# Moving two output projections into their attentions' buffers, new buffers at the end of the latent stage, and a later transpose of the softmax maxima, in a two-layer diffusion backbone on one Trainium2 core

## The chip, the cores and the metric

The kernel runs on one core of a Trainium2 chip. A core has a matrix engine (TensorE, PE in the profile, with its weight loads shown apart as PEld), a vector engine (DVE), an activation engine (ACT), a general engine (POOL), and a queue engine (SP) that here issues transfers only. ACT and POOL issue some transfers too. Operands lie in an on-chip memory (SBUF), the matrix engine writes into accumulator banks (PSUM), and everything larger lives in device memory. The metric is the device time of one execution in microseconds (us), as the median of several runs. Three runs of the kernel before took 3708.83, 3715.74 and 3721.25 us, so its median is 3715.74 us.

## What is computed

The reference is a network of two layers over 2048 latent tokens on a grid 64 wide, with 256 context tokens ahead of them; a token has 1024 channels. Both layers normalize and modulate, project, mix, gate, project again and add to the stream:

```python
for i in range(DEPTH):                     # 2 layers
    h  = rms_norm(x,  norm_g[i]) * (1 + scale)   + shift
    hc = rms_norm(cx, norm_g[i]) * (1 + c_scale) + c_shift
    y, yc = even_mixer(...) if i % 2 == 0 else odd_mixer(...)
    x = x + gate * y
    if i < DEPTH - 1:                      # the context is updated by layer 0 only
        cx = cx + c_gate * yc
```

Layer 0 (even) has two heads' groups side by side: latent attention (8 heads, queries and keys of 96 elements made from low-rank latents, softmax over all 2304 tokens for latent queries and over the 256 context tokens for context queries) and a gated linear attention (4 heads, run in both directions). Layer 1 (odd) is a neighbourhood attention (16 heads, a window of 8 rows by 16 columns plus all context tokens). Both end with a product by a 1024 x 1024 matrix: `readout(...)` in layer 0 for 18 tiles of 128 tokens (2 of context, 16 latent), and `jnp.dot(o * silu(z), w_out)` in layer 1 for the 16 latent tiles.

## The kernel before, in words

All is in float32. A product is made of three matmuls on operands split into a high and a low part: high by high, high by low, low by high. Lines 120 to 122 and 129 to 131 issue them. The split of an operand is one copy on ACT (the high part) and one subtraction on DVE (the low part); `project_split` (line 1059) does it for a projection. Tokens come in 18 tiles of 128, of which tiles 0 and 1 are context.

The stages, with their times in the profiled execution:

- `even_latent`, to about 549 us. For each tile it makes the latents (`gemm`), then queries, keys and values from them (`up`: transposes at line 495 into the tag "tp", splits into `lth` and `ltl`, products into `qn`, `kn` and `vn`, and a chain of squares, sums and powers on ACT, DVE and POOL that normalizes `qn` and `kn`), and one step later transposes queries and keys (`fin`, line 549), splits them into `qkhl` (two buffers) at lines 106 and 553, and stores them to the device tensors `QT` and `KT`. At its end `first` computes four column blocks of the next stage's products, evicts each into the one buffer `vn` and stores it to `Un`.
- `even_rest`, to about 1099 us. The rest of layer 0's input products run as the main generator of `weave`, in steps of three matmuls; beside them the side generator `maxes` computes, head by head, all scores of the attention once (line 651) and reduces them to row maxima (line 652). After a head, its maxima are reduced to `mc` (line 655), transposed on PE (line 657), negated into `mr` and stored by POOL as one more row of `QT`, so that the attention can subtract them inside its product. `weave` starts the side after `head` main steps (20) and then issues 1.06 side steps for each main step.
- `even_mix`, to about 1981 us: both attentions of layer 0, in pools `atS` (SBUF) and `atP` (PSUM). `finish` (line 833) ends a block of 512 queries: a product that sums the softmax denominators (`den`, line 838), a logarithm and an exponential on ACT, three DVE operations, one on POOL, and a store to `RT`.
- The output projection of layer 0, to about 2197 us, by `project` (line 1080) in new pools `woS` and `woP`: `project_load` reads a tile of `RT` and of the stream, `project_split` splits it into `prh` and `prl`, `project_steps` issues 48 matmuls of 512 columns, multiplies by the gate on DVE (line 1072), adds on POOL (line 1073), and stores.
- `odd_qk` and `odd_vz`, to about 3110 us: the input products of layer 1. In `odd_vz` again a side generator `maxes` computes score maxima (line 1280, reductions at 1275 and 1286), with a transpose of `mc` at line 1293 and four stores by POOL for each head.
- `odd_attention`, to about 3498 us. The projections of its first two output tiles are issued inside its pools, to about 3527 us.
- The other 14 tiles by `project` in new pools `wpA`, `wpS` and `wpP`, to the end. Here `project_load` also reads the gate path `z` and POOL multiplies it in (line 1056).

The order of the work on an engine is the order in which the program issues it, except where a block asks for another place with `issue_after`, and the planner of the framework places instructions of a generator by priority. Buffers of a tag are reused in turn; whoever writes one next waits for its last reader. New pools that take the memory of earlier ones wait for those in the same way.

Of the kernel before, what the change touches and what calls it, by code (L numbers as in the profile page):

```python
# [10 lines left out]
F32 = mybir.dt.float32  # L11
# [77 lines left out]
class Kern:  # L89
# [303 lines left out]
    def even_latent(self, ws, wrest, kept):  # L393
# [5 lines left out]
        with ExitStack() as es:  # L399
# [87 lines left out]
            def up(t):  # L487
# [3 lines left out]
                for g in range(2):  # L491
                    ps = self.tl(pp, [P, 4, P], "tp")
# [49 lines left out]
            def fin(t):  # L542
                qn, kn = nat.pop(t)
                for z, (src, dst) in enumerate(((qn, self.QT), (kn, self.KT))):
                    col = 2 * z + (0 if t < NCT else 1)
                    for h2 in range(2):
                        ps = self.tl(pp, [P, 4, P], "tp")
                        for j in range(4):
                            nc.tensor.transpose(ps[:A_QK, j, :], src[:, h2 * 4 + j, :], self.ident[:])
                        hl = self.tl(sp, [P, 4, 2, P], "qkhl", F32R, bufs=2)  # L550
# [9 lines left out]

            def first(t, j):
                (hi, lo), (wh, wl) = kept[t], wrest[j]
                ps = self.tl(pp, [P, LAT_CHUNK], "gm", bufs=2)
                self.mm3(ps[:], (lambda k: hi[:, k, :], lambda k: lo[:, k, :]),
                         (lambda k: wh[:, k, :], lambda k: wl[:, k, :]), range(KD))
                u = self.tl(sp, [P, LAT_CHUNK], "vn", bufs=1)
                self.act(u[:], ps[:])
                nc.scalar.dma_start(self.Un[t, :, (j - 2) * LAT_CHUNK : (j - 1) * LAT_CHUNK], u[:])
# [31 lines left out]
    def even_rest(self, ws, win, hT):  # L600
        nc = self.nc
        self.zaT = self.scr("zaT", (4, P, T), F32)
        with ExitStack() as es:
# [33 lines left out]
            def maxes():  # L637
                for h in range(A_HEADS):
# [4 lines left out]
                    for t in range(NT):  # L643
# [4 lines left out]
                        for n, k0 in enumerate(range(0, lim, 512)):  # L648
# [4 lines left out]
                            yield mm  # L653
                    mc = self.tl(sp, [P, NT], "mc", bufs=1)
                    nc.vector.tensor_reduce(out=mc[:], in_=m[:], axis=AX.X, op=ALU.max)
                    ps = self.tl(pp, [P, 512], "mx", bufs=5)
                    mm = nc.tensor.transpose(ps[:NT, :P], mc[:], self.ident[:])
                    r = self.tl(sp, [P, P], "mr", F32R, bufs=1)
                    self.act(r[:NT], ps[:NT, :P], AF.Copy, scale=-1.0)
                    nc.gpsimd.dma_start(self.QT[h, 0, A_QK].rearrange("(t p) -> t p", p=P), r[:NT].bitcast(F32))  # L660
                    yield mm

            self.weave(gemms, maxes(), 1.06, 30, 20)
# [169 lines left out]
    def finish(self, av, dacc, zt, dst, w, ap, pp, tag, lnp=None, bufs=(1, 2), out=None):  # L833
# [3 lines left out]
        for h in range(2):  # L837
            nc.tensor.matmul(den[h * 64 : h * 64 + 64, :w], self.mtwos[:], dacc[h], start=True, stop=True)
# [12 lines left out]
    def even_attention(self, ap, pp):  # L851
# [4 lines left out]
        ring = [self.tl(ap, [P, 2, W], f"akh{n}", F32R, bufs=1) for n in range(4)]  # L856
        for kh in ring:
            nc.gpsimd.memset(kh[A_QK : A_QK + 1].bitcast(F32), 1.0)
# [65 lines left out]
        for j in range(4):  # L924
# [12 lines left out]
            for nb, (q0, w, kts) in enumerate(blocks):  # L937
# [18 lines left out]
                for n, kt in enumerate(kts):  # L956
# [21 lines left out]
                    if nb == 4 and j < 3 and n % TT == TT - 1 and n < NT - 1:  # L978
                        load(keys(j + 1, n // TT + 1), low(j + 1, n // TT))
        while pend:  # L980
# [10 lines left out]
    def even_mix(self, e1, win, hT):  # L991
# [3 lines left out]
        with ExitStack() as es:  # L995
            with ExitStack() as esa:
# [26 lines left out]
                for n, _ in enumerate(att):  # L1023
                    if n == 18:
                        pre = {t: self.project_load(self.RT, t, t, self.i["xin"], ld) for t in range(2)}
# [13 lines left out]
            gate = [self.gate_load(0, c, self.tl(sp, [P, D], f"gate{c}", bufs=1)[:]) for c in range(2)]  # L1039
            self.project(0, self.RT, [(t, t) for t in range(NT)], self.i["xin"], self.x1, w, sp, pp, ld, pre, gate, ahead=ahead())  # L1040
# [39 lines left out]
    def project(self, l, RT, tiles, xsrc, dst, w, sp, pp, ld, pre, gate, z=None, ahead=iter(())):  # L1080

        for t, o in tiles:
# [3 lines left out]
            for _ in self.project_steps(hi, lo, x, gate[1 if t < NCT else 0], w, lambda: self.tl(pp, [P, 512], "pj", bufs=4),  # L1086
# [127 lines left out]
    def odd_vz(self, ws, win, hT):  # L1214
# [3 lines left out]
        with ExitStack() as es:  # L1218
# [31 lines left out]
            def maxes():  # L1250
                for h in range(16):
# [11 lines left out]
                    for R in range(16):  # L1263
# [19 lines left out]
                        for ro, ri, rn in pieces("q", 0, g, r0, nr):  # L1283
                            for co, ci, cn in pieces("q", 1, c, c0, w):
# [3 lines left out]
                                n += 1  # L1288
                        yield mm
                    mc = self.tl(mp, [P, 16], "mc", bufs=1)  # L1290
                    nc.vector.tensor_reduce(out=mc[:], in_=m[:], axis=AX.X, op=ALU.max)
                    pt = self.tl(pp, [P, 512], "mx", bufs=5)
                    nc.tensor.transpose(pt[:16, :P], mc[:], self.ident[:])
                    r = self.tl(mp, [P, P], "mr", F32R, bufs=1)
                    self.act(r[:16], pt[:16, :P], AF.Copy, scale=-1.0)
                    for g in range(4):
# [402 lines left out]
```

## Time and profile before

| what | value |
|---|---|
| median of three runs | 3715.74 us |
| the profiled execution | 3709.59 us |
| its span on the core | 3707.8 us |
| PE busy | 3566.3 us (96%) |
| DVE busy | 2374.2 us (64%) |
| ACT busy | 1438.5 us (39%) |
| POOL busy | 1209.2 us (33%) |
| mean granted PE clock | 0.982 |

The span is the time from the first to the last instruction; the execution lasts 1.8 us longer. A view by windows gives each engine's busy time in a stretch; the timeline lists instructions with start and duration, and in square brackets the idle time of the engine ahead of one and what released it; the list of waits sums these by pair. Matmuls overlap, so the step from one start to the next, and not the duration shown, is what one costs.

### The profile page before, as it was taken

Reading aid. Unit: us, or ns where it says so; the run is one execution under the profiler, and the core shown is the slowest. Engines: PE = TensorE matmul, PEld = TensorE weight load, DVE = VectorE, ACT = ScalarE, POOL = GpSimd, SP = SyncE. Lnnn points to the kernel's source line nnn. Section 1 sums busy time; section 2 is a strip of 40 time slices with the busy share of each in tenths; the row PEclk is TensorE's granted clock in tenths of the full one; section 3 lists DMA queues with packets and bytes.
Section 4 is the critical chain, followed back from the end, with each engine's and each line's share of the span. In section 5 each row is a group of like instructions: output and inputs, shape, how many; then the busy total and the mean of one; then the engine's idle time right before and its main releaser. Section 6 shows DMA issues by size and latency. Waiting matters only on the chain.

```text
span 3707.8 us, 51752 instructions
## 1 busy us (share of the span) xinstructions
PE 3566.3 (96%) x18404; PEld 2754.6 (74%) x18404; DVE 2374.2 (64%) x4860; ACT 1438.5 (39%) x2741; POOL 1209.2 (33%) x1336
## 2 busy tenths in 40 slices
PE   7999989999999999999999999999899999999889
PEld 6988988888886666655656878888688887555567
DVE  4677656888876666697665344545478773666722
ACT  5545541111115555555553124444322223555400
POOL 1433420111111212122201233333344443777743
PEclk9999999999999999999999999999999999999999
DMA  7455453222242232334514543445744437887564
GB/s 257 138 164 160 129 170 98 87 75 85 75 127 63 82 97 79 91 105 121 163 55 151 165 149 117 150 142 175 215 143 123 136 117 200 216 215 205 162 195 130
DMA packets 364372, 512.18 MB, mean 138 GB/s; under 512 B 25826, under 2 KB 243890, under 8 KB 358211
## 3 DMA queue, kind: packets, MB, share of 16 engines
q1 hardware_dynamic: 322642, 425.49, 39.0%
q0 software_dynamic: 19872, 55.92, 5.1%
q10 hardware_dynamic: 21600, 27.46, 2.1%
q8 instruction: 146, 2.39, 0.3%
q14 instruction: 112, 0.91, 0.1%
HBM read 329.38 MB, written 179.37 MB: 137 GB/s over the span
## 4 chain that ended last, share of the span: by engine, by line
PE 79%; DVE 7%; DMA 6%; POOL 3%; ACT 3%; issue 2%; SPq 0%; POOLq 0%; ACTq 0%; DVEq 0%
PE gm L129 9%; PE gm L130 9%; PE gm L131 9%; PE av L905 7%; PE st L963 4%; PE mx L651 4%; PE st L964 3%; PE st L965 3%; PE pj L129 3%; PE pj L130 3%; PE pj L131 3%; PE o L1406 2%; PE st L1373 1%; DMA wraw<-w_od 1%; PE mx L1280 1%
## 5 line engine op out<-in xcount | busy, mean ns | idle before, releaser
L954 DVE TENSOR_TENSOR acc<-acc,apt 128x512 f32<-128x512 f32 x512 | 364.6, 737 | 158.3 <-ACT apt L106 155.4
L106 ACT ACTIVATE apt<-st 128x512 f32<-128x512 f32 (+1 forms) x592 | 344.4, 594 | 284.3 <-PE st L965 247.2
L652 DVE TENSOR_REDUCE mm<-mx 128x1 f32<-128x512 f32 (+1 forms) x656 | 389.3, 629 | 81.3 <-PE mx L651 74.4
L905 PE MATMUL av<-apt,av 128*64 128x512 f32 (+1 forms) x1184 | 288.0, 600 | 0.0
L963 PE MATMUL st<-aq,akh 97*128 97x512 f32 (+1 forms) x592 | 254.0, 429 | 5.1 <-ACT apt L106 2.8
L651 PE MATMUL mx<-mk,mq 96*128 96x512 f32 (+1 forms) x656 | 236.8, 373 | 6.1 <-DMA mq<-QT 4.6
L964 PE MATMUL st<-aq,akh 96*128 96x512 f32 (+1 forms) x592 | 235.2, 397 | 0.0
L965 PE MATMUL st<-aq,akl 96*128 96x512 f32 (+1 forms) x592 | 234.0, 396 | 0.0
L1286 DVE CUSTOM_DVE_ANT_1 mx<-mx,mtab 128x225 f32<-128x225 f32 (+12 forms) x576 | 183.7, 339 | 58.1 <-PE mx L1280 42.7
L106 ACT ACTIVATE u<-gm 128x352 f32<-128x352 f32 (+1 forms) x140 | 68.6, 497 | 369.4 <-PE gm L131 208.0
L905 PEld LDWEIGHTS av<-apt,av 128*64 128x64 f32 x1184 | 82.1, 138 | 157.1 <-issue 155.8
L1537 DVE TENSOR_TENSOR opt<-st,tab 128x64 f32<-128x64 f32 (+10 forms) x576 | 142.7, 316 | 86.6 <-PE st L1374 58.3
L963 PEld LDWEIGHTS st<-aq,akh 97*128 97x128 f32 x592 | 112.3, 190 | 98.4 <-issue 43.7
L1412 POOL TENSOR_TENSOR oacc<-oacc,opt 128x682 f32<-128x682 f32 (+9 forms) x144 | 169.6, 1206 | 23.2 <-ACT opt L106 21.9
L1073 POOL TENSOR_TENSOR px<-py,px 128x512 f32<-128x512 f32 x64 | 86.4, 1350 | 232.8 <-DVE py L1072 232.8
L106 ACT ACTIVATE opt<-opt 128x930 f32<-128x930 f32 (+8 forms) x130 | 104.4, 805 | 106.2 <-DVE opt L1537 102.3
L106 ACT ACTIVATE prh<-pr 128x1024 fp32r<-128x1024 f32 x32 | 33.9, 1058 | 263.1 <-PE pj L130 235.6
L651 PEld LDWEIGHTS mx<-mk,mq 96*128 96x128 f32 x656 | 121.7, 189 | 17.6 <-issue 5.0
L965 PEld LDWEIGHTS st<-aq,akl 96*128 96x128 f32 x592 | 113.6, 192 | 25.5
L964 PEld LDWEIGHTS st<-aq,akh 96*128 96x128 f32 x592 | 113.9, 192 | 18.0
L1373 PE MATMUL st<-q,kt 128*128 128x480 f32 (+5 forms) x256 | 99.0, 389 | 25.8 <-DVE opt L1537 20.9
L106 ACT ACTIVATE x<-px,modB,modA 128x128 f32<-128x128 f32 x272 | 99.3, 469 | 57.2 <-PE px L331 50.9
(517 smaller groups left out, 10069.0 us busy)
## 6 DMA issues: line engine op xcount, KB each, us to landing
q<-Q SPq DMA_DIRECT2D x48, 512.0 KB
H<-x ACTq DMA_DIRECT2D x36, 512.0 KB
adaw<-ada_w SPq DMA_DIRECT2D x64, 256.0 KB
x<-H SPq DMA_DIRECT2D x32, 512.0 KB
pr<-RT SPq DMA_DIRECT2D x32, 512.0 KB
wraw<-w_od SPq DMA_DIRECT2D x64, 256.0 KB
K1t<-okt POOLq DMA_DIRECT2D x32, 512.0 KB, 7.6
kt<-K1t SPq DMA_DIRECT2D x32, 512.0 KB
```

The costliest lines, as they stand in the source:

```text
L106: return self.nc.scalar.activation(out, in_, func, **kw)
L129: self.nc.tensor.matmul(out, lh(k), rh(k), start=j == 0, stop=False)
L130: self.nc.tensor.matmul(out, lh(k), rl(k), start=False, stop=False)
L131: yield self.nc.tensor.matmul(out, ll(k), rh(k), start=False, stop=j == n - 1)
L651: mm = nc.tensor.matmul(ps[:, :w], q[:A_QK, (t % 6) * P : (t % 6) * P + P], k[:A_QK, k0 : k0 + w], start=True, stop=True)
L652: nc.vector.tensor_reduce(out=m[:, t, n : n + 1], in_=ps[:, :w], axis=AX.X, op=ALU.max)
L905: nc.tensor.matmul(O[j, nb][i * 64 : i * 64 + 64, :w], V[j, kt // TT][:, kt % TT, i * 64 : i * 64 + 64], pts[i][:, :w], start=n == 0, stop ...
L954: nc.vector.tensor_tensor(out=acc[i][:, :w], in0=a[:, :w], in1=pts[i][:, :w], op=ALU.add)
L963: nc.tensor.matmul(ps[:, :w], kh[: A_QK + 1, i, kq], qh[: A_QK + 1, :w], start=True, stop=False)
L964: nc.tensor.matmul(ps[:, :w], kh[:A_QK, i, kq], ql[:A_QK, :w], start=False, stop=False)
L965: mm = nc.tensor.matmul(ps[:, :w], kl[:A_QK, i, kq], qh[:A_QK, :w], start=False, stop=True)
L1286: nc.vector.tensor_tensor_reduce(out=s, in0=s, in1=tb[:, ri : ri + rn, ci : ci + cn], scale=1.0, scalar=-3e38, op0=ALU.add, op1=ALU.max, a ...
```

## The change

It has four parts.

1. *End of the latent stage.* For the last tile, `up` transposes into the bank tag "px" and not "tp". `fin` of the last tile takes the keys first and puts their halves into `lth` and `ltl`, with transposes in "px"; the queries follow in "tp" and `qkhl`. `first` evicts into slices of a tile of the tag "u", three to a tile, and not into the one buffer `vn`.
2. *Maxima.* In both `maxes` the transpose of a head's maxima, its negation and its stores are put into a function `post`, called inside the next head (after its tile 3 in layer 0, at row block 4 in layer 1), and after the loop for the last head. In `even_rest` the side generator starts after 32 main steps, not 20.
3. *Layer 0's output projection.* Tiles 0 and 1, the context, are computed with the attention's buffers: the gate in `ring[0]`, the halves in the tag "aq", the banks "gl" and "st", the result in "rc". Nine of their matmuls stand ahead of the attention's last value products, the others behind the last `den`. Tile 2's loads are issued ahead of the new pools; `project` does tiles 2 to 17.
4. *Layer 1's output projection.* All tiles are computed inside the attention's pools. Operands of a tile come from the ring of the tag that `exps` takes, fetched two tiles ahead (`fetch`), multiplied and split one tile ahead (`ready`). The pools `wpA`, `wpS` and `wpP` are gone.

The diff, cut:

```diff
@@ even_latent: up, fin, first
-                    ps = self.tl(pp, [P, 4, P], "tp")
+                    ps = self.tl(pp, [P, 4, P], "px" if t == NT - 1 else "tp")
...
-                for z, (src, dst) in enumerate(((qn, self.QT), (kn, self.KT))):
+                both = [(0, qn, self.QT), (1, kn, self.KT)]
+                for z, src, dst in both[::-1] if t == NT - 1 else both:
...
-                        ps = self.tl(pp, [P, 4, P], "tp")
+                        ps = self.tl(pp, [P, 4, P], "px" if z and t == NT - 1 else "tp")
...
-                        hl = self.tl(sp, [P, 4, 2, P], "qkhl", F32R, bufs=2)
+                        if z and t == NT - 1:
+                            hl = self.tl(sp, [P, 8, P], ("lth", "ltl")[h2], F32R, bufs=1)[:].rearrange("p (j s) t -> p j s t", s=2)
+                        else:
+                            hl = self.tl(sp, [P, 4, 2, P], "qkhl", F32R, bufs=2)
...
+            spare = []
             def first(t, j):
+                if not spare:
+                    x = self.tl(sp, [P, LAT_COLS], "u", bufs=2)
+                    spare.extend(x[:, n * LAT_CHUNK : (n + 1) * LAT_CHUNK] for n in range(3))
...
-                u = self.tl(sp, [P, LAT_CHUNK], "vn", bufs=1)
-                self.act(u[:], ps[:])
+                u = spare.pop(0)
+                self.act(u, ps[:])
@@ even_rest: maxes (odd_vz alike, with "if R == 4 and post: post()")
+                        if t == 3 and post:
+                            yield post()
                     mc = self.tl(sp, [P, NT], "mc", bufs=1)
                     nc.vector.tensor_reduce(out=mc[:], in_=m[:], axis=AX.X, op=ALU.max)
+                    def post(h=h, mc=mc):
...
+                        return mm
+                yield post()
-            self.weave(gemms, maxes(), 1.06, 30, 20)
+            self.weave(gemms, maxes(), 1.06, 30, 32)
@@ even_mix
+                early = []
+                for n, last in enumerate(att):
                     if n == 18:
-                        pre = {t: self.project_load(self.RT, t, t, self.i["xin"], ld) for t in range(2)}
+                        gate = self.gate_load(0, 1, self.att_free[:].rearrange("p i w -> p (i w)")[:, :D].bitcast(F32))
+                        for t, tag in zip(range(NCT), (("gl", 2), ("st", 3))):
+                            r, x = self.project_load(self.RT, t, t, self.i["xin"], ld)
+                            hl = self.tl(ap, [P, 4, 512], "aq", F32R, bufs=2)
...
+                    elif n == 19:
+                        self.project_split(again[0][:], *again[1:])
+                        with self.tc.issue_after(last.ins):
+                            for _ in range(3):
+                                mm = next(early[0])
+                        break
+                with self.tc.issue_after(mm.ins):
+                    for _ in att:
+                        pass
+                with self.tc.issue_after(self.den.ins):
+                    for steps in early:
+                        for _ in steps:
+                            pass
+                pre = {NCT: self.project_load(self.RT, NCT, NCT, self.i["xin"], ld)}
@@ odd_attention
+            def fetch(o):
+                z, r, x = exps([P, KD, P]), exps([P, KD, P]), exps([P, D])
+                rows(z, self.z1, o, all_k)
+                rows(r, self.RT1, o, all_k)
+                self.load(x[:], self.x1[tok(o), :])
+                return z, r, x
+            def ready(z, r, x, parts=None):
+                nc.gpsimd.tensor_tensor(out=r[:], in0=r[:], in1=z[:], op=ALU.mult)
+                hi, lo = parts or [exps([P, KD, P], F32R) for _ in range(2)]
+                self.project_split(r[:], hi[:], lo[:])
+                return hi, lo, x
...
+            got[1] = ready(*got[1], parts)
+            for o in range(1, NT - NCT):
+                if o + 1 < NT - NCT:
+                    nxt = ready(*got.pop(o + 1))
+                if o + 2 < NT - NCT:
+                    got[o + 2] = fetch(o + 2)
+                for _ in steps_of(o, *got.pop(o)):
+                    pass
+                got[o + 1] = nxt
@@ odd_tail
-            ld, sp = [self.pool(es, n, bufs=2, side="left", reuse_waits="tile") for n in ("wpA", "wpS")]
-            pp = self.pool(es, "wpP", bufs=2, space=PSUM, reuse_waits="tile")
-            self.project(1, self.RT1, [(t, t - NCT) for t in range(NCT + 2, NT)], self.x1, out, w, sp, pp, ld, {}, [gate], self.z1)
```

71 lines of the change are left out of this document (38 added, 33 removed).

## The prediction

> **What bounds the kernel now.** I read the page first, then PE's waits, then windows, then the timeline around each wait.
>
> ```profile
> PE 3566.3 (96%) x18404; PEld 2754.6 (74%) x18404; DVE 2374.2 (64%) x4860; ACT 1438.5 (39%) x2741; POOL 1209.2 (33%) x1336
> PE 79%; DVE 7%; DMA 6%; POOL 3%; ACT 3%; issue 2%; SPq 0%; POOLq 0%; ACTq 0%; DVEq 0%
> ```
>
> PE is busy 96% of the span, the chain that ended last lies on it for 79%, and the change leaves its number of matmuls as it is. So a gain can only come out of PE's idle time, 3707.8 − 3566.3 = 141.5 us, and out of matmuls that run slowly after a stall. The windows show where idle time lies near the edits (columns: stretch, its length, busy time of PE, PEld, DVE, ACT and POOL, granted PE clock, DMA share, GB/s).
>
> ```profile
> 520.00:560.00 40.00, 30.19 (x166) 27.70 (x165) 18.76 (x30) 16.53 (x26) 6.58 (x7) 0.87 0.57 162
> 600.00:1060.00 460.00, 459.47 (x2395) 407.89 (x2394) 381.93 (x644) 59.99 (x107) 45.80 (x79) 1.00 0.23 74
> 2720.00:3040.00 320.00, 314.60 (x1555) 262.92 (x1555) 253.59 (x1064) 83.78 (x140) 145.45 (x122) 1.00 0.42 135
> 3520.00:3560.00 40.00, 27.28 (x108) 21.63 (x107) 8.44 (x10) 3.17 (x3) 16.45 (x10) 0.83 0.72 204
> 3560.00:3700.00 140.00, 139.22 (x599) 111.92 (x597) 43.16 (x37) 11.66 (x11) 56.05 (x35) 1.00 0.50 156
> ```
>
> Where PE idles, its clock is below 1 as well (0.87, 0.83). The last row gives the full pace of a 512-column matmul, 139.22 / 599 = 0.232 us.
>
> **A. End of the latent stage.** PE's waits from 500 to 600 us, and three places of its timeline (start, duration, idle time before it and its releaser):
>
> ```profile
> PE gm L120 <- ACT vn L106: 6.6, 1, 6.6
> PE mx L651 <- DMA mq<-QT: 4.6, 1, 4.6
> PE tp L495 <- DVE qkhl L553: 3.5, 2, 2.8
> PE tp L549 <- DVE qkhl L553: 3.2, 3, 1.2
> PE mx L651 <- DVE mm L652: 1.5, 1, 1.5
> ```
> ```profile
> 511.49 1.12 PE L495 MATMUL tp<-ident,u 128*128 128x128 f32 x4 [2.80 <-DVE qkhl L553]
> 549.48 0.41 PE L129 MATMUL gm<-W2h,hhi 128*128 128x352 f32 x1
> 565.57 0.55 PE L651 MATMUL mx<-mk,mq 96*128 96x256 f32 x1 [4.56 <-DMA mq<-QT]
> ```
>
> Ahead of the next stage's first matmul (549.48) PE waits 6.6 + 3.5 + 3.2 = 13.3 us: for `qkhl`, whose two buffers wait for their stores to land, and for the one buffer `vn`. The edits give each another buffer or bank. From 508.69 (where the 2.80 us begin) to 549.48 are 40.8 us. I estimate slow matmuls after these stalls at 4.2 us, so the work itself is 23.3 us. Without stalls PE reaches `fin` of the last tile, which is the last 2.2 us of that work, at 508.69 + 21.1 = 529.8. There a wait that was hidden appears: the keys `kn` of this tile.
>
> ```profile
> 521.86 0.49 ACT L106 ACTIVATE qn<-up 128x384 f32<-128x384 f32 x1 [6.84 <-PE up L122]
> ```
> ```profile
> 536.32 1.46 POOL L537 TENSOR_TENSOR kn<-kbase,sqk 128x256 f32<-128x256 f32 x1
> ```
> ```profile
> 553.99 0.75 DVE L553 SCALAR_TENSOR_TENSOR qkhl<-tp,qkg,qkhl 96x512 fp32r<-96x512 f32 x1 [0.42 <-ACT qkhl L106]
> ```
>
> `kn` is ready at 537.8, 15.9 us after the eviction of `qn` began. The eviction moves up by the 3.5 us of waits and about 1.6 us of slow matmuls ahead of it, hence `kn` to 532.7. Behind this wait on PE stand the transposes of `fin` and all of the next stage. So: wait to 532.9, 2.2 us of transposes, about 1 us for a bank to be evicted, and about 1.5 us of slow pace, the first matmul of the next stage at 537.6 and not 549.48: **−11.9 us**. Bounds: −16 (no wait, no slow pace) and −8 (`kn` as late as 536.5, if the DVE work that stands ahead of it, the splits of the next weights, waits for their transfer).
>
> Then the maxima. PE waits 4.6 + 1.5 us there, and I estimate 1.7 us of slow pace: 7.8 us. From the last split (553.99) to the first score matmul (565.57) stores, loads and waits take 11.6 us. After the change the last split comes at about 540, so the operands are there at 551.6. The head of 32 steps is 16 of three 352-column and 16 of three 512-column matmuls, about 19 us, so the first score is due at 556.6: covered by 5 us. With 20 steps it would be due at 548 and wait. **−7.8 us**, bounds −8 and −3.
>
> **B. Start of the attention.** The head of 32 also moves the end of the maxima. By the order in which the instructions stand, 39 matmuls lay between the last transpose of `mc` and the first `st` (39 × 0.232 = 9.0 us ahead of 1099.26); now three do, 0.7 us. On POOL the store of this row stands ahead of the clearing of `akh`, for which the first `st` waits.
>
> ```profile
> 1027.34 0.28 PE L657 MATMUL mx<-ident,mc 128*18 128x128 f32 x1
> 1099.26 0.28 PE L963 MATMUL st<-aq,akh 97*128 97x256 f32 x1
> 1101.85 0.38 PE L963 MATMUL st<-aq,akh 97*128 97x256 f32 x1 [1.36 <-ACT apt L106]
> ```
> ```profile
> 1028.21 0.52 POOL L660 DMA_DIRECT2D QT<-mr  x1 [4.18 <-ACT mr L106]
> 1096.12 5.34 POOL L858 MEMSET akh<- 1x1536 f32 x4
> ```
>
> From a transpose to the end of that store's issue are 1028.73 − 1027.34 = 1.4 us, one clearing is 5.34 / 4 = 1.3 us, and about 0.1 us brings it to PE: 2.8 us less the 0.7 us of cover, and about 0.4 us in which the transpose waits for `mc`, so a new wait of 2.5 us. In it ACT gets its table load done, whose wait of 1.36 us goes. **+1.1 us**, bounds 0 and +3.
>
> **C. Layer 0's projection.** Columns as above.
>
> ```profile
> 1980.33 1.08 PE L838 MATMUL den<-acc,mtwos 128*64 128x512 f32 x4
> 1983.78 0.50 PE L129 MATMUL pj<-gu,prh 128*128 128x512 f32 x1 [2.37 <-ACT prh L106]
> 1987.56 0.80 PE L129 MATMUL pj<-gu,prh 128*128 128x512 f32 x1 [2.57 <-ACT prh L106]
> 1992.39 0.40 PE L129 MATMUL pj<-gkt,prh 128*128 128x512 f32 x1
> ```
> ```profile
> 1873.49 0.43 SPq L1047 DMA_DIRECT2D pr<-RT  x1
> ```
> ```profile
> 1982.69 1.04 ACT L106 ACTIVATE prh<-pr 128x1024 fp32r<-128x1024 f32 x1
> ```
>
> After `den` (end 1981.41) PE does 15 matmuls by 1992.39, 3.5 us of work in 11.0 us: 7.5 us are lost, 4.9 of them waiting for `prh` behind the last `finish`. After the change 87 context matmuls, 20 us, cover it. They need loads issued at 1873 already, over 100 us earlier, and per tile a split of 1.04 us on ACT and a subtraction of like length on DVE, put between exponentials; neither engine is the bound here. New is a wait at tile 2: its `prl` stands behind POOL's last addition of tile 1. From the last context matmul to that split's end I count 0.7 (DVE, as in the row 3699.33 below) + 1.3 (POOL, row 3599.60 below) + about 1.2 (the split) + some 0.8 between, 4.0 us; eight matmuls (1.9 us) stand ahead. So 2.1 us come back: **−5.4 us**, bounds −7 and −1.
>
> **D. The maxima's transposes.** PE's waits from 2660 to 3110 us:
>
> ```profile
> PE mx L1293 <- DVE mc L1291: 6.4, 10, 1.8
> ```
>
> In the next head `mc` is long done. DVE is not the limit (253.59 of 320 us), though later transposes keep their buffers longer. POOL's four stores for a head move with them, with nothing urgent behind. In the even stage PE has only 0.5 us idle (600 to 1060). **−6.0 us**, bounds −7 and 0.
>
> **E. Layer 1's projection.** PE, then the chain, then DVE at the end:
>
> ```profile
> 3527.20 0.40 PE L131 MATMUL st<-kc,oacc 128*128 128x512 f32 x1
> 3540.32 0.80 PE L129 MATMUL pj<-wo,prh 128*128 128x512 f32 x1 [12.72 <-ACT prh L106]
> ```
> ```profile
> 3530.57 6.11 DMA pr<-RT
> 3536.84 2.35 POOL pr L1056
> ```
> ```profile
> 3699.33 0.69 DVE L1072 TENSOR_TENSOR py<-pj,kt 128x512 f32<-128x512 f32 x1 [4.89 <-PE pj L131]
> ```
>
> The new pools wait for the old, so load, product and split of the next tile follow tile 1, and PE waits 12.72 us and runs slowly after. Fourteen tiles of 48 matmuls are 672 × 0.232 = 156 us, yet from 3527.4 to the end of the matmuls at about 3699 are 171.5: 15 us are lost. With tile 2 fetched and split ahead (I place its halves at 3515, from its POOL product at about 3508.5) they go: **−15 us**, bounds −16 and −8, the latter if that preparation delays `finish` of the attention's last block. The last matmul, DVE, POOL and store to the end stay.
>
> In the steady state SP now issues a tile's store, then the next load into the ring, which waits until that store has landed; POOL's product waits for the load, and POOL's next addition stands behind the product.
>
> ```profile
> 3600.93 0.35 SPq L1074 DMA_DIRECT2D out_dram<-px  x1
> 3603.89 0.33 SPq L1054 DMA_DIRECT2D px<-x  x1
> 3546.12 0.36 SPq L1047 DMA_DIRECT2D pr<-RT  x1
> ```
> ```profile
> 3599.60 1.30 POOL L1073 TENSOR_TENSOR px<-py,px 128x512 f32<-128x512 f32 x1 [1.59 <-DVE py L1072]
> 3550.38 2.40 POOL L1056 TENSOR_TENSOR pr<-pr,pz 128x1024 f32<-128x1024 f32 x1 [1.34 <-DMA pr<-RT]
> ```
>
> A store's buffer is loaded anew 2.96 us after the store was issued, a load is used 4.26 us after its issue: 2.96 + 4.26 + 2.40 + 1.30 and about 0.7 between, a loop of 11.6 us beside 48 × 0.232 = 11.1 us of PE. Half a microsecond per tile over 13 tiles is 6 us, inside the lead of about 16 us that a tile prepared from two tiles back has. Cost nothing, but with little room.
>
> **Sum.** −11.9 − 7.8 + 1.1 − 5.4 − 6.0 − 15 = −45 us, so 3709.6 − 45.0 = 3664.6 us for an execution like the profiled one. That one is 6.1 us under the median, 3715.74, so I forecast **3670 us**.
>
> [...] After the 2.57 us wait matmuls step from 1987.56 to 1992.39 at 0.43 us and not 0.232: a wait costs more than its length. [...]
>
> **The rivals.**
> - *The latent end keeps its chain.* If the weight splits hold `kn` back and the query stores still land late, the first score waits again: 4 us are gained in place of 19.7, 3670 + 15 = **3685 us**. For it: POOL's `kn` today ends only 11.7 us before 549.48. Against: it starts from the eviction of `qn`, which moves.
> - *The tail's loop is the bound (slower).* If store and load each take the 6.11 us that the crowded load took, the loop is 2 × 6.11 + 2.40 + 1.30 + 0.7 = 16.6 us, 5.5 us over PE's 11.1. Over 13 tiles that is 71 us, less the lead of 16: 55 us, **3725 us**. It cancels the gain from a loop of about 15.8 us on. Against: 2.96 and 4.26 us at a DMA share of 0.50, and a loaded volume per tile that stays.
> - *The waits only move.* If each removed wait comes back at the next resource (bank, DVE, store), nothing changes: **3715 us**. Against: four places with different releasers would all have to do so; 600 to 1060 us shows a weave with no idle time.
>
> [...]
>
> **How the numbers follow.** Chances: forecast 0.66, latent chain 0.17, no change 0.07, slower tail 0.10. A difference of 0.3% (11 us) is about what runs that spread from 3708.83 to 3721.25 can tell from none. So faster 0.83, same 0.07, slower 0.10. The forecast's own range is the sum with all best ends, 3709.6 − 54, to all worst, 3709.6 − 17, each plus 6: 3662 to 3699. Single runs spread by 6 us. The range from 3655 to 3698 takes in the latent chain and leaves out the two cases without a gain.
>
> **What would show it.** Right: the first W2 matmul near 537.6 with one wait on `kn`; no wait at the first score; 2.5 us on POOL at the first `st`; no L1293-like waits in the odd stage; no idle time at 3527 and a last matmul about 156 us after tile 1. Wrong: idle PE time every 11 us in the tail with releaser ACT or POOL; `kn` after 536; new waits inside layer 0's attention for the early splits.

## The result

| kernel | median of runs | lowest to highest | runs |
|---|---|---|---|
| before | 3718.49 us | 3708.83 to 3721.26 | 4 |
| after | 3663.68 us | 3656.81 to 3676.20 | 4 |

The ratio is 0.9865, with a 95% interval from 0.985 to 0.988. In two later series, each with its own runs of the kernel before, it was 0.9884 (0.9865 to 0.9903) and 0.9875 (0.9855 to 0.9896). So the change takes 44 to 55 us off. The forecast was 3670 us, 45.7 us under the median known then. The total came out near the forecast. One of its terms did not, and that is what most of the experiments are about.

The profiled execution of the kernel after took 3676.2 us, the longest of its four runs. The page's busy times and its chain, which answer to the first two lines shown in the prediction:

```profile
PE 3565.7 (97%) x18404; PEld 2758.7 (75%) x18404; DVE 2363.0 (64%) x4860; ACT 1437.0 (39%) x2741; POOL 1205.6 (33%) x1336
PE 69%; issue 15%; POOL 5%; DVE 5%; DMA 4%; ACT 2%; SPq 0%; POOLq 0%; DVEq 0%; ACTq 0%
```

PE has as many matmuls and as much busy time as before (3565.7 against 3566.3 us), in a span of 3674.1 in place of 3707.8 us. The gain is idle time alone, as it had to be. The windows around the edits (length, busy PE, PEld, DVE, ACT, POOL, clock, DMA share, GB/s):

```profile
520.00:560.00 40.00, 34.16 (x185) 30.42 (x183) 19.19 (x31) 16.22 (x25) 7.12 (x8) 0.96 0.86 243
2700.00:3020.00 320.00, 318.03 (x1573) 267.05 (x1572) 256.78 (x1070) 84.70 (x142) 145.39 (x122) 0.99 0.44 136
3485.00:3525.00 40.00, 40.00 (x195) 30.48 (x192) 14.28 (x19) 8.48 (x11) 20.46 (x14) 1.00 0.61 191
3525.00:3665.00 140.00, 139.12 (x599) 112.13 (x598) 28.93 (x36) 10.68 (x11) 55.99 (x36) 1.00 0.54 165
```

Where layer 1's projection starts, PE was busy for 27.28 of 40 us at a clock of 0.83. Now it is busy for all 40 at 1.00. In the window at the latent stage's end PE is busy for 34.16 us, where it was 30.19. PE's waits of the kernel after, from 500 to 600 us (total, times, longest):

```profile
PE tp L634 <- DVE u L628: 4.4, 1, 4.4
PE px L550 <- POOL kn L537: 3.2, 1, 3.2
```

All five waits of before, 19.4 us, are gone. In their place stand the wait on `kn` that the prediction names, and one that it does not. The timeline shows where:

```profile
534.69 1.94 PE L550 MATMUL px<-ident,kn 128*96 128x128 f32 x8 [3.23 <-POOL kn L537]
538.19 0.43 PE L129 MATMUL gm<-W2h,hhi 128*128 128x352 f32 x1 [0.18 <-DVE ltl L557]
557.18 0.40 PE L661 MATMUL mx<-mk,mq 96*128 96x256 f32 x2
561.93 1.12 PE L634 MATMUL tp<-ident,u 128*128 128x128 f32 x4 [4.36 <-DVE u L628]
1085.96 0.39 PE L980 MATMUL st<-aq,akh 97*128 97x256 f32 x1 [1.90 <-POOL akh L875]
```

The first matmul of the next stage starts at 538.19 (549.48 before, forecast 537.6), and the first score at 557.18 without a wait (forecast 556.6). But 4.4 us later PE stops for 4.36 us at a transpose of `u`. No part of the prediction has that wait.

To compare kernels I cut each trace at the same instructions. The fourth row takes the second and third together, with the first 62 `st` matmuls of the attention, because its slow start belongs to what happened ahead of it:

| stretch (us) | before | after | after, 2nd | after, 3rd | forecast of the change |
|---|---|---|---|---|---|
| start to first W2 matmul | 549.5 | 538.2 | 536.4 | 538.0 | −11.9 |
| W2 to first `st` | 549.8 | 547.8 | 549.0 | 548.2 | |
| first to 62nd `st` | 21.2 | 23.1 | 20.2 | 23.2 | |
| W2 to 62nd `st` | 571.0 | 570.9 | 569.2 | 571.4 | −7.8 + 1.1 |
| last `den` of layer 0 to its last projection matmul | 205.8 | 198.6 | 198.6 | 198.7 | −5.4, with the 9 matmuls moved ahead |
| from there to layer 1's first score | 480.4 | 475.1 | 474.5 | 478.5 | none |
| first score to first `st` of layer 1 | 446.3 | 441.8 | 442.1 | 440.6 | −6.0 |
| last run of `o` matmuls of layer 1 (its start) to the last matmul | 194.8 | 180.5 | 179.4 | 179.4 | −15 |

### The profile page after: what moved, and what is told of

It is laid out like the page before. It is cut to its first block, busy times and chain, and to the rows that moved or that the text cites. A ratio compares the mean times of both kernels' runs of the same rounds, so it can differ in the third digit from the quotient of the medians.

```text
span 3674.1 us, 51831 instructions
## 1 busy us (share of the span) xinstructions
PE 3565.7 (97%) x18404; PEld 2758.7 (75%) x18404; DVE 2363.0 (64%) x4860; ACT 1437.0 (39%) x2741; POOL 1205.6 (33%) x1336
## 4 chain that ended last, share of the span: by engine, by line
PE 69%; issue 15%; POOL 5%; DVE 5%; DMA 4%; ACT 2%; SPq 0%; POOLq 0%; DVEq 0%; ACTq 0%
PE av L922 7%; PE gm L129 6%; PE gm L130 6%; PE gm L131 6%; PE st L980 4%; PE st L981 4%; PE st L982 4%; PE st L129 2%; PE st L131 2%; PE st L130 2%; PE pj L131 2%; PE pj L130 2%; PE pj L129 2%; PE o L1456 2%; DMA wraw<-w_od 1%
## 5 line engine op out<-in xcount | busy, mean ns | idle before, releaser
L1330 DVE CUSTOM_DVE_ANT_1 mx<-mx,mtab 128x217 f32<-128x217 f32 (+11 forms) x576 | 184.6, 338 | 49.2 <-PE mx L1324 37.9
L106 ACT ACTIVATE opt<-opt 128x930 f32<-128x930 f32 (+9 forms) x144 | 119.2, 830 | 248.0 <-POOL opt L1627 141.0
L1462 POOL TENSOR_TENSOR oacc<-oacc,opt 128x682 f32<-128x682 f32 (+10 forms) x144 | 169.8, 1199 | 26.4 <-ACT opt L106 25.1
L129 PE MATMUL gm<-w0h,hhi 128*128 128x512 f32 x288 | 116.1, 403 | 0.0
L129 PE MATMUL gm<-w1h,hhi 128*128 128x512 f32 x288 | 115.7, 402 | 0.0
```

Of the source, the lines that this page charges most:

```text
L106: return self.nc.scalar.activation(out, in_, func, **kw)
L129: self.nc.tensor.matmul(out, lh(k), rh(k), start=j == 0, stop=False)
L1330: nc.vector.tensor_tensor_reduce(out=s, in0=s, in1=tb[:, ri : ri + rn, ci : ci + cn], scale=1.0, scalar=-3e38, op0=ALU.add, op1=ALU.max, a ...
```

## The experiments

Every kernel here computes the whole output. The first four each undo one part of the change by taking the functions of the kernel before.

### One part undone

*The tail* (`odd_attention` and `odd_tail` as before):

```diff
-            for o in range(1, NT - NCT):
-                if o + 1 < NT - NCT:
-                    nxt = ready(*got.pop(o + 1))
...
+            ld, sp = [self.pool(es, n, bufs=2, side="left", reuse_waits="tile") for n in ("wpA", "wpS")]
+            pp = self.pool(es, "wpP", bufs=2, space=PSUM, reuse_waits="tile")
+            self.project(1, self.RT1, [(t, t - NCT) for t in range(NCT + 2, NT)], self.x1, out, w, sp, pp, ld, {}, [gate], self.z1)
```

> The change without its part 4 (layer 1's projection as before, 14 tiles in new pools). My theory: the wait of 12.7 us at the first of the 14 tiles comes back with its slow matmuls, the stretch from the last value product of the odd attention to the last matmul is about 195 us again and not 180.5, and the ratio to the kernel before is 0.9865 + 15/3716 = 0.9905 (0.989 to 0.992). Rival: the loads for the tail, fetched during the odd attention, slow that attention (it took 396.0 us in the changed kernel's profile, 390.1 before); then that stretch goes back to 390 and only about 8 us are lost, 0.9887.

Measured: 3684.85 us (3681.50 to 3687.90), ratio 0.9919 (0.9902 to 0.9936). PE's waits from 3480 to 3560 us:

```profile
PE pj L129 <- ACT prh L106: 12.9, 1, 12.9
```

The old wait is back, and the stretch from the last run of `o` to the last matmul takes 195.0 us, 14.5 to 15.6 more than in the kernel after.

*The context projection* (`even_mix` and `project` as before):

```diff
-                            hl = self.tl(ap, [P, 4, 512], "aq", F32R, bufs=2)
...
+                        pre = {t: self.project_load(self.RT, t, t, self.i["xin"], ld) for t in range(2)}
```

> The change without its part 3 (layer 0's projection of the context as before, in new pools). My theory: two waits of 2.4 and 2.6 us for the split tile come back after the last denominators, with slow matmuls, and the ratio is 0.9865 + 5.4/3716 = 0.988. Rival: the early splits in the attention and the loads ahead cost as much there as they save (the attention took 5.1 us longer in the changed kernel's profile, 3 us beyond its 9 added matmuls); then the attention takes 882 us again and the ratio stays at 0.9865 to 0.987.

Measured: 3681.01 us (3675.85 to 3686.11), ratio 0.9908 (0.9891 to 0.9924). PE's timeline after the last `den`:

```profile
1971.76 0.50 PE L129 MATMUL pj<-gu,prh 128*128 128x512 f32 x1 [2.37 <-ACT prh L106]
1975.54 0.80 PE L129 MATMUL pj<-gu,prh 128*128 128x512 f32 x1 [2.59 <-ACT prh L106]
```

These are the two waits shown in the prediction (2.37 and 2.57 us). The stretch takes 206.2 us as in the kernel before, not 198.6.

*The latent stage's end* (`even_latent` as before, the head of 32 kept):

```diff
-                u = spare.pop(0)
-                self.act(u, ps[:])
+                u = self.tl(sp, [P, LAT_CHUNK], "vn", bufs=1)
+                self.act(u[:], ps[:])
```

> The change without its part 1 (end of the latent stage as before, the head of 32 steps kept). My theory: the first matmul of the next stage is at 549.5 again (538.2 with the change), the score operands still come in time, and 11 us are lost: ratio 0.9895. Rival: the new wait of 4.4 us that the changed kernel has at the first transposes of the next stage is the price of the earlier start (the weights come late), and goes with it; then only about 7 us are lost, 0.9884.

Measured: 3695.94 us (3692.59 to 3699.84), ratio 0.9948 (0.9933 to 0.9963). PE's waits from 500 to 600 us:

```profile
PE tp L625 <- DVE u L619: 6.7, 1, 6.7
PE gm L120 <- ACT vn L106: 6.0, 1, 6.0
PE tp L495 <- DVE qkhl L553: 4.0, 2, 3.0
PE tp L549 <- DVE qkhl L553: 3.2, 3, 1.2
```

The first W2 matmul starts at 552.6. The three old waits are back with 13.2 us. The wait on `u` (line 619 here) is there too, and longer than in the kernel after. So it comes neither from the new buffers nor from the earlier start.

*The late transposes* (`maxes` of both layers with the transpose in its own head, the head of 32 kept):

```diff
-                        if t == 3 and post:
-                            yield post()
...
+                    mm = nc.tensor.transpose(ps[:NT, :P], mc[:], self.ident[:])
...
+                    yield mm
```

> The change with the maxima transposed in their own head again in both layers (the head of 32 steps kept). My theory: ten waits of 6.4 us together come back in the odd input stage and none in the even stage, so the stretch from the first to the last score matmul there takes 415 us and not 410, and the ratio is 0.988. Rival: DVE is what those waits stood for; then the waits show at other places with the change and undoing it costs nothing, ratio 0.9865.

Measured: 3694.66 us (3689.97 to 3697.65), ratio 0.9943 (0.9928 to 0.9958). In the odd stage the old waits come back (447.3 us in place of 441.8). The surprise is the even stage, 560.5 us from W2 to the first `st` in place of 547.8. PE's waits there:

```profile
PE mx L666 <- DVE mc L664: 9.0, 6, 2.3
```

In the kernel before, these transposes had no wait to speak of (0.5 us idle from 600 to 1060 us). I had written that moving them is worth nothing there.

Of these four ratios only the tail's lies in the range that was expected. The others are higher by more than their intervals: 0.9908 for 0.988, 0.9948 for 0.9895 and 0.9943 for 0.988. Together the four losses come to 68 to 96 us, reckoned from the kernel after at 0.9884 or 0.9865, while the whole change gains 44 to 55. So the parts don't add. The even stage with own-head transposes is one piece of the surplus. The rest stays open, since the kernel after did not run beside these four.

### Is the late transpose of value by itself, or only with a head of 32?

Transposes of the even stage in their own head, with the head of 20; all else as in the kernel after:

```diff
-            self.weave(gemms, maxes(), 1.06, 30, 32)
+            self.weave(gemms, maxes(), 1.06, 30, 20)
```

> The changed kernel with the even input stage's maxima transposed in their own head, and the head of 20 steps, as in the kernel before (the odd stage's transposes stay late). It asks why undoing the late transposes cost 9 us of waits in the even stage with a head of 32, where the kernel before had none. Theory: the head decides, by the place at which a head's last maxima meet other DVE work; then there is under 1 us of waits for mc here. Rival: it is the earlier start of the stage; then 5 us or more of them are here too.

Measured, in one run: 3681.51 us. W2 to the first `st` takes 547.4 us, and no transpose waits for `mc`. DVE ahead of the first transpose, first with the head of 32 (the kernel with own-head transposes), then with 20. With 32 this transpose waits 0.31 us; the fifth waits longest, 2.29 us:

```profile
639.80 4.00 DVE L661 TENSOR_REDUCE mm<-mx 128x1 f32<-128x512 f32 x7
643.83 0.25 DVE L664 TENSOR_REDUCE mc<-mm 128x18 f32<-128x90 f32 x1
```
```profile
637.30 0.43 DVE L661 TENSOR_REDUCE mm<-mx 128x1 f32<-128x256 f32 x1 [0.56 <-PE mx L660]
637.76 0.25 DVE L664 TENSOR_REDUCE mc<-mm 128x18 f32<-128x90 f32 x1
```

With 32, seven reductions follow each other without a gap; DVE is behind, and `mc` comes late. With 20, each reduction waits for its score. The traces show why. In the first case, the head's last scores stand among matmuls of 352 columns, and a score follows the one before it by about 0.72 us (three matmuls and a score). DVE takes 4.00 / 7 = 0.57 us for a reduction and has its other work beside that. In the second case, they stand among matmuls of 512 columns, and a score comes every 0.92 us. Of the seven heads that end among 352-column matmuls in the run with 32, six wait; the last, among 512-column ones, does not. The later start moved the heads' ends to where DVE is short. The late transpose then repairs what the head of 32 broke. With a head of 20 it is worth about 2 us (547.4 against 545.3 us below), one trace on each side.

### Does the head have to be 32?

```diff
-            self.weave(gemms, maxes(), 1.06, 30, 32)
+            self.weave(gemms, maxes(), 1.06, 30, 20)
```

Two kernels ran beside each other, the kernel after once more and this one.

> The changed kernel itself, a second time, as the common base for the runs beside it and to tell what in its first profile was chance. My theory: the attention of layer 0 (887.2 us in the first profile, 882.1 before) and the odd attention (396.0, 390.1 before) were long by chance beyond 2 us for the 9 added matmuls: a second profile shows at least one of them shorter by 2 us or more, and the ratio is within 0.985 to 0.990. Rival: both lengths are the change's own and come again.

> The changed kernel with the side work starting after 20 main steps in the even input stage, not 32. My theory: the score operands then come too late, PE waits 3 to 5 us at the first score matmul, while the wait of 1.9 us at the first score of the attention goes, since 39 matmuls lie there again; in all 2 to 4 us slower than the change, the stage from its first matmul to the attention's first at 549 to 552 us (547.8 with 32). Rival: the head is not what hides them, since the weights come late anyway; then the stage takes 547 us or less.

Measured: 3665.13 us (3660.53 to 3676.06) for the kernel after, ratio 0.9884; 3666.15 us (3664.06 to 3669.49) with 20, ratio 0.9882 (0.9865 to 0.9898). They are the same, and my theory of a loss of 2 to 4 us falls. The theory for the repeat holds: its two attentions are 8.0 and 5.7 us shorter than in the first trace, so their length there was in large part chance, and no sign that the tail's loads slow them. PE's waits with 20, from 500 to 1200 us:

```profile
PE px L550 <- POOL kn L537: 3.6, 1, 3.6
PE mx L661 <- DMA mq<-QT: 1.9, 1, 1.9
PE st L980 <- ACT apt L106: 1.4, 1, 1.4
```

The first score does wait, for 1.90 us, as the argument of the prediction wants. But the 4.4 us at `u` are gone: the scores that now start at 551.89 are PE's work while it would wait there. The stage takes 545.3 us, 2.5 to 3.7 less than with 32.

At the attention's start there is a second difference. Columns as above, the kernel after and then this one:

```profile
1080.00:1120.00 40.00, 37.85 (x159) 23.93 (x158) 21.78 (x36) 20.91 (x38) 8.49 (x12) 0.91 0.36 102
```
```profile
1080.00:1120.00 40.00, 38.64 (x180) 25.44 (x179) 22.82 (x37) 24.44 (x47) 8.89 (x12) 1.00 0.42 121
```

With 32, PE waits 1.90 us for `akh`. From 1087.54 to 1093.9 its matmuls then run slowly, those of 512 columns at steps of 0.426 us and not 0.232, so the first 62 `st` take 23.1 in place of 21.2 us. The granted clock was 0.50 from 1088 to 1092 us and 1.00 from 1096 to 1100. Of the eight traces with this wait, only the second one of the kernel after shows no slow step behind it (20.2 us, with a granted clock of 1.00 from 1080 to 1108 us). A wait of 1.54 us, in the two runs below that store the last maxima from ACT's queue, is followed by about 3 us of slow steps in one and by none in the other. What decides this, no run here shows.

### What holds `u`, and can it be freed?

The new wait in the kernel after can be followed through three engines. ACT, DVE and the queue SP:

```profile
558.97 1.06 ACT L106 ACTIVATE wr1h<-wraw 128x1024 fp32r<-128x1024 f32 x1 [12.32 <-DMA wraw<-w_rest]
559.93 0.58 ACT L106 ACTIVATE u<-gm 128x512 f32<-128x512 f32 x1
```
```profile
544.10 0.23 DVE L652 MEMSET mm<- 128x90 f32 x2 [4.33 <-DMA QT<-qkhl]
544.28 2.36 DVE L383 TENSOR_TENSOR wr1l<-wraw,wr1h 128x1024 fp32r<-128x1024 f32 x2
560.06 1.23 DVE L383 TENSOR_TENSOR wr1l<-wraw,wr1h 128x1024 fp32r<-128x1024 f32 x1 [13.42 <-ACT wr1h L106]
561.20 0.68 DVE L628 SCALAR_TENSOR_TENSOR u<-u,gm 128x512 f32<-128x512 f32 x1
```
```profile
543.98 1.94 SPq L656 DMA_DIRECT2D mq<-QT  x2
545.96 0.64 SPq L650 DMA_DIRECT2D mk<-KT  x1
546.64 1.42 SPq L380 DMA_DIRECT2D wraw<-w_rest  x2
```

Read from the end: `u` stands on ACT and on DVE behind a split of the next weights, `wr1`. That split waits 12.3 us for its load. The load was issued at 546.64, when the split before it ended (544.28 + 2.36) and gave the buffer back, and behind the scores' operands on the queue. That split could not start because the clearing of `mm`, whose buffer lies on `qkhl`, waits on DVE for the query stores until 544.10.

But the weights are no later than they were. This split starts 558.97 − 538.19 = 20.8 us after the stage's first matmul. The same split in the kernel before, and in the one with the old latent end:

```profile
571.32 1.06 ACT L106 ACTIVATE wr1h<-wraw 128x1024 fp32r<-128x1024 f32 x1 [13.35 <-DMA wraw<-w_rest]
```
```profile
574.53 1.06 ACT L106 ACTIVATE wr1h<-wraw 128x1024 fp32r<-128x1024 f32 x1 [13.51 <-DMA wraw<-w_rest]
```

They start 21.8 and 21.9 us after that matmul (549.48 and 552.59). With a head of 20, PE has scores to do, or waits for them, in this time. With 32 it comes to `u` first. With the old and the new latent end the wait on `u` is 0 and 0.2 us at a head of 20, and 6.7 and 4.4 us at 32. So it is the price of the head of 32, and not of the earlier start.

*The cure:* issue the later loads of `wr1` from ACT's queue, and clear `mm` of the first two heads on POOL:

```diff
-                self.wload = nc.sync.dma_start(w[:], src[:, s, c])
+                self.wload = (nc.scalar if tag == "wr1" and k0 >= 4 else nc.sync).dma_start(w[:], src[:, s, c])
...
-                    nc.vector.memset(m[:], -3e38)
+                    (nc.gpsimd if h < 2 else nc.vector).memset(m[:], -3e38)
```

I first ran it together with an edit against the wait for `akh`, and that edit also alone. It stores the last row of maxima from ACT's queue, so that POOL's clearing does not stand behind it:

```diff
-                        nc.gpsimd.dma_start(self.QT[h, 0, A_QK].rearrange("(t p) -> t p", p=P), r[:NT].bitcast(F32))
+                        (nc.scalar if h == A_HEADS - 1 else nc.gpsimd).dma_start(self.QT[h, 0, A_QK].rearrange("(t p) -> t p", p=P), r[:NT].bitcast(F32))
```

> The changed kernel with the last head's row of maxima stored from ACT's queue and not from POOL's, so that POOL clears the attention's key buffers earlier. My theory: the wait of 1.9 us at the attention's first score matmul goes to 0.4 us or less, or is replaced by up to 1.4 us for ACT's first exponentials behind the table load; nothing else moves, 1 to 2 us less, too little for the times to tell. Rival: POOL was not what it waited for, and the wait stays.

> As the run before it, and the second half of the weights of the even input stage loaded from ACT's queue, ahead of the second head's keys, with the clearing of the first two heads' maxima on POOL and not on DVE. My theory: those loads are issued at about 543 us and not 546.6, land before 555 and not at 558.9, and the wait of 4.4 us at the first transposes of that stage goes, with about 1 us of slow matmuls: the stage takes 541 to 544 us from its first matmul to the attention's first (547.8 before). Rival: the loads take 12 us however early they are, since the score operands share the DMA engines; then the wait only shrinks by the 3 us that they start earlier.

Measured: the store alone 3680.38 us (3675.56 to 3682.37), ratio 0.9919 (0.9904 to 0.9933), 15 us slower than the kernel after beside it. With the cure 3672.06 us (3671.11 to 3678.25), ratio 0.9902 (0.9887 to 0.9916). The wait for `akh` does go. In its place PE waits in the attention. PE's waits from 500 to 1200 us, and SP's from 1040 to 1100, both with the store alone:

```profile
PE gl L722 <- POOL gu L721: 13.7, 1, 13.7
```
```profile
SPq L885 <- DMA QT<-mr: 29.3, 1, 29.3
```

SP issues nothing from 1052.5 to 1081.86: by the profile the load of `akh` waits 29.3 us for the moved store, which is issued at 1080.60. In the kernel after (second run) that load is issued at 1055.16. It needs nothing from that store, for it reads `KT` and the store writes `QT`. Why it waits for that store was not shown. All of SP's loads for the attention stood behind it. With the cure in addition, the stage from W2 to the first `st` takes 539.9 us and the wait on `u` is gone, but the 15.3 us in the attention stay.

*The cure alone*, beside the kernel after for a third time, and with a head of 24:

```diff
-            self.weave(gemms, maxes(), 1.06, 30, 32)
+            self.weave(gemms, maxes(), 1.06, 30, 24)
```

> The changed kernel once more, the base for the two runs beside it: ratio to the kernel before 0.985 to 0.990, the even input stage 547 to 549 us from its first matmul to the attention's first.

> The changed kernel with the second half of the weights of the even input stage loaded from ACT's queue and the first clearings of maxima on POOL; the last row of maxima is stored from POOL again. My theory: the wait of 3 to 4 us at the first transposes goes as it did with the ACT store, and the wait of 14 us in the linear attention, which came with that store, does not come: the stage takes 541 to 543 us, the attention 879 to 887, in all 6 us less than the change (ratio to it 0.9975 to 0.999). Rival: the transfers on ACT's queue are what delayed the attention's loads; then a wait over 10 us in the linear attention comes here too.

> As the run before it, with a head of 24 steps. My theory: the score operands come at about 552, the first score is due at 537 + 16 x 0.48 + 8 x 0.70 = 550.5, a wait of 1 to 2 us; the wait of 1.9 us at the attention's first score goes or turns into 1.4 us for ACT: the stage takes 540 to 542 us, within 1.5 us of the head of 32. Rival: the operands come as early as the weights now do; then there is no wait at the first score, and the stage is 2 us shorter than with 32.

Measured: the kernel after 3670.92 us (3666.04 to 3675.66), ratio 0.9875; the cure 3663.41 us (3659.06 to 3666.74), ratio 0.9851 (0.9828 to 0.9874); with a head of 24 3666.85 us (3665.34 to 3670.83), ratio 0.9866 (0.9847 to 0.9885). ACT, DVE and PE with the cure:

```profile
545.00 1.73 ACTq L380 DMA_DIRECT2D wraw<-w_rest  x2
555.09 1.06 ACT L106 ACTIVATE wr1h<-wraw 128x1024 fp32r<-128x1024 f32 x1 [6.54 <-DMA wraw<-w_rest]
```
```profile
557.33 0.68 DVE L628 SCALAR_TENSOR_TENSOR u<-u,gm 128x512 f32<-128x512 f32 x1
```
```profile
559.30 0.60 PE L634 MATMUL tp<-ident,u 128*128 128x128 f32 x4
```

The first of the two loads is there at 555.09, 15.0 us after the stage's first matmul and not 20.8, `u` is ready at 558.0, 1.3 us ahead of its transpose, and PE does not wait. W2 to the first `st` takes 541.9 us against 548.2 in the kernel after beside it, 6.3 us less. The medians differ by 7.5 us, in the same direction, though the two intervals overlap. Of the versions tried this has the lowest ratio. Of its two edits neither ran alone. The stage and the attention (883 us) are as expected, and no long wait in the linear attention comes with the loads on ACT's queue, so that rival falls. The head of 24 takes away the wait for `akh` but lets the first score wait 2.75 us, more than the 1 to 2 expected, and the stage takes 544.5 us in place of 540 to 542; to the 62nd `st` it takes 565.7 us, with 32 it takes 564.9.

## Why the prediction was right, and where it was not

**A, the latent stage's end: right.** −11.9 forecast, −11.3, −13.1 and −11.5 us in the three traces. The wait on `kn` took the place of the others until 534.69 (forecast 532.9), while what stands behind it, with a granted clock of 0.57 from 534 to 538 us, took less time than I gave it: 3.5 us from the end of the wait to the first W2 matmul, forecast 2.2 + 1 + 1.5 = 4.7. Undone, the waits came back one for one (13.2 us for 13.3).

**A's second part and B, the maxima's start and the attention's start: wrong.** The step that failed is "covered by 5 us ... **−7.8 us**", with "**+1.1 us**" behind it. The first half holds, for the score itself does not wait. I looked only at the instruction whose wait I removed. What the same 32 steps of the main stream need was not asked: their own transposes need `u`, and `u` stands behind weights that are loaded only after the scores' operands. The lost time came back as 4.36 us (3.1 to 4.5 over three traces) at line 634, with slow matmuls behind it: in the first trace the five from 562.70 take 2.23 us, where five at 0.232 take 1.16. At the attention the wait was 1.90 us (forecast 2.5), but slow pace follows it, and the first 62 `st` take 1.9 us more (23.1 against 21.2). From W2 to the 62nd `st`, the forecast was −6.7 us and the traces show −0.1, −1.8 and +0.4. That is the rival "the waits only move", at this one place. The cure shows the cause: with the weights' path freed and the head still 32, the wait is gone and the stretch is 6.1 us shorter than in the kernel before.

**C, the context projection: right.** The stretch after `den` is 7.2 us shorter, of which 9 matmuls (2.1 us) are work that was moved ahead of it: −5.1 us, forecast −5.4. PE's waits there, from 1900 to 2100 us:

```profile
PE pj L131 <- DVE prl L1104: 1.0, 1, 1.0
PE pj L129 <- DVE rc L1115: 0.4, 1, 0.4
```

The wait at tile 2 for `prl`, foretold with 2.1 us, is there with 1.0, and 0.4 us for `rc` stand ahead of it.

**D, the transposes: right for layer 1, half right for layer 0.** −4.5, −4.2 and −5.7 us for −6.0, and all waits at the transposes are gone. In layer 0, "only 0.5 us idle" was true of the kernel before. But with the head of 32 the same transposes would wait 9.0 us. I priced two edits one at a time that act on each other.

**E, the tail: right, with less room than I saw.** −14.3, −15.4 and −15.4 us for −15. In the first trace, the waits of PE from 3440 us to the end hold one that belongs to the tail. After it stand two lines of POOL's timeline, its products of two tiles that are ten apart:

```profile
PE st L129 <- DVE rc L1115: 0.9, 1, 0.9
```
```profile
3521.58 2.39 POOL L1627 TENSOR_TENSOR opt<-opt,opt 128x1024 f32<-128x1024 f32 x1 [4.80 <-DMA opt<-RT]
3648.77 2.40 POOL L1627 TENSOR_TENSOR opt<-opt,opt 128x1024 f32<-128x1024 f32 x1 [6.25 <-DMA opt<-RT]
```

The loop takes (3648.77 − 3521.58) / 10 = 12.7 us a tile, not 11.6, beside about 11.1 of PE. The terms that were too small are the first two of the loop's sum: from a store to the load issued behind it 4.0 us on average and not 2.96, from that load to its use 4.9 and not 4.26. So 1.6 us of the lead go with each tile, and it is used up just at the last one, where the wait lies (3654.28). The other two traces of this kernel show no wait there; the kernel with the old latent end waits at the last two tiles, 0.5 and 1.9 us. The slower rival named the right mechanism. It fails because there are only 14 tiles: with some more, by this count, PE would wait in each. No run here has more.

**The sum.** The terms come to −11.3 − 0.1 − 5.1 − 4.5 − 14.3 = −35 us in the first trace and to −13.1 − 1.8 − 5.1 − 4.2 − 15.4 = −40 in the second. The spans of these traces are 33.7 and 49.4 us shorter than that of the kernel before; the medians show −55, −45 and −45. What the terms leave lies in stretches that no edit was to shorten: layer 1's input products took 480.4 us before and 474.5 to 478.5 after (483.4 with own-head transposes and 20), and layer 0's attention spreads by 8 us between traces of the same kernel. With one trace of the kernel before I can't say whether any of that belongs to the change. So the total was hit partly by luck: the miss at B (−6.7 us forecast, +0.4 to −1.8 measured) and this rest cancel.

## What to carry to other kernels

When a wait at an instruction is removed by letting other work go first, ask what that other work needs, not only whether the waiting one is now covered: here one queue of loads fed both, and the wait came back at the next consumer with 4.36 us. Two edits at one place are to be priced together, since the start of a side stream decides where its heads end, and so whether a late step is worth nothing or 9 us. A loop that is slower than the bound costs nothing only as long as its lead lasts; divide the lead by the loss per turn, and compare with the number of turns.

## What was not expected of the hardware

- A wait of 1.90 us was followed, 1.6 to 2.4 us later, by 3 to 7 us of matmuls at a little over half pace (in the first trace 0.426 us a step and not 0.232), in seven of the eight traces with that wait. A wait of 1.36 us at the same place was followed by none in all four traces that have it.
- With a store moved to ACT's queue, a load on SP's queue that needs nothing from it waited 29.3 us for it by the profile, and this kernel was 15 us slower than the kernel after beside it. What ties the two was not shown.
- A load of weights issued behind the scores' operands took 12.3 us from 546.64 to its use at 558.97; in the window from 520 to 560 us the DMA engines were busy to 0.86 and moved 243 GB/s.
